# Sums on VectorE in a hybrid decoder step: the first feature pair's weight sums and the squares of x

## The chip, the cores and the metric

The kernel runs on one core of one Trainium2 chip. The metric is the device time in microseconds (us) of one execution; of several runs the median is given. In the text, PE is TensorE (PEld its weight loads), DVE is VectorE, ACT is ScalarE, POOL is GpSimd, and SP is SyncE, which here only issues DMAs.

## The reference

One layer of a conditioned decoder runs for a prompt of 1024 rows and for 8 samples of 4 rows, which the kernel joins to R = 1056 columns of a transposed x (1024 features in 8 tiles of 128 partitions). Cut to what matters here:

```python
h = rmsnorm(x, g_norm1) * (1 + scale1) + shift1
za, zq, zkv, zg, zm = jnp.split(h @ w_in, SPLIT_IDX, axis=-1)
...                                        # gMLP mixer, sparse attention, output projection
x = x + gate1 * mixed
h2 = rmsnorm(x, g_norm2) * (1 + scale2) + shift2
up = h2 @ w_up                             # 1024 -> 2 * 2816
conv = b_conv
for k in range(CONV_W):                    # causal depthwise convolution, width 3
    conv = conv + w_conv[k] * upc[:, k:k + T]
a, gv = jnp.split(conv, 2, axis=-1)
x = x + gate2 * ((jax.nn.gelu(a) * gv) @ w_down)
```

All inputs and outputs are float32. Before these lines a conditioning vector gives shift, scale and gate, and after them a last RMSNorm follows.

## The kernel before

**Precision and weights.** A float32 product is made from parts: `split` copies a tile into a rounded high part (ACT) and subtracts it for the low part (DVE), and each product of two tiles is three matmuls (high by high, high by low, low by high). A product with float32 operands, such as the row sums, leaves two records for each matmul in the trace. Weight tiles come through three rings of 128x512 buffers: `raw` (6 buffers, filled by `raw_load` on SP's queue), `hi` and `lo` (4 each). `weights(src, 8)` takes two raw buffers and two of each other ring.

**Order.** Except for PE in one part in the middle, a scheduler puts the instructions of each engine in order at build time: it runs a timeline of its own simulation (`schedule_with_timeline_sim=True`) and prefers what stands earlier in the program. Each engine then works its list off in that order, and waits on semaphores for data and for buffers.

**Statistics of x.** x is cut into three chunks of columns, CH = 0:384, 384:768, 768:1056. `x_stats(c)` squares the eight tiles of a chunk (ACT, L328), adds the squares over the features and turns the sums into factors: `row_sums` multiplies 128-column pieces of each tile handed to it with a column of ones (PE, one column of output), `rstd_rows` makes 1/sqrt by a few small DVE steps (L286 to L305), spreads them by transposes on PE (L294), and ACT copies them to RB (L333). Before `row_sums`, chunk 0's squares are added up by DVE and chunk 2's by POOL (L330) into the first tile, so that one tile is handed on; chunk 1's eight tiles are handed on as they are. `x_mult(c)` multiplies x by RB (L338; POOL for two tiles in eight, DVE for the rest), `h_tile` scales, shifts and splits the tiles (L390 to L398), and `rows(2, ...)` multiplies them with the first weights. The loop runs over the chunks: `h_tile` of chunk c, then `x_stats` and `x_mult` of chunk c + 1, then `rows` of chunk c.

**Up projection.** The 22 feature pairs (one tile of a, one of gv) are computed by a scheme of seven block products on halves of rows (HR = 528 columns), features and outputs, as in Winograd's form of fast matrix multiplication. The activations need the combined operands T1 to T4, B22 and the plain ones in BS, made once (`sums_of`, `turned`: ACT casts L1625, DVE subtracts L1626, DVE sums L1634, L1635, L1653, L1656). The weights of a pair need the sums s1 to s4 of its four raw 128x512 blocks a11, a12, a21, a22: `pair_weights(j)` loads these and `add_up` forms the sums (L1546 to L1549), on POOL for all pairs. For pair 0 the sums live in two `acc` tiles and `add_up` is called apart from the load.

Before pair 0 stands a preparation: `first_products(j)` makes two of the block products of pairs 0 to 3 ahead, with weights loaded by `weights` into `early[0]` to `early[3]`, and ACT copies them out of PSUM (L1533). Between them `sums_of` is called four times. Then `pair(j)` runs for all pairs: products with s2, s3, a22, s1 and s4 (and two more from pair 4 on), DVE adds of the banks into the tiles ua and ug (L1569, L1583, L1595 to L1598), the convolution (L1521 to L1523), gelu (L1607), a product on POOL (L1608) and the store.

Of the kernel before, what the change touches and what calls it, by code (L numbers as in the profile page):

```python
# [11 lines left out]
OP = mybir.AluOpType  # L12
# [38 lines left out]
def step_kernel(tc, A):  # L51
    nc = tc.nc
    sync, act, dve, pool, pe = nc.sync, nc.scalar, nc.vector, nc.gpsimd, nc.tensor
# [211 lines left out]
    def row_sums(pv, ts):  # L265

        w = ts[0].shape[1]
        for i in range(-(-w // 128)):
            n = min(128, w - 128 * i)
            for k, t in enumerate(ts):  # L270
                m = mm(pv[0:n, i:i + 1], t[:, 128 * i:128 * i + n], ones, k == 0, k == len(ts) - 1)
        return m
# [51 lines left out]
    def x_stats(c):  # L324
        a, b = CH[c]
        sq = [R0([128, 384], F32, "sq", 8)[:, 0:b - a] for k in range(8)]
        for k in range(8):
            act.activation(sq[k], xs[k][:, a:b], AF.Square)  # L328
            if c != 1 and k:
                (pool if c else dve).tensor_tensor(sq[0], sq[0], sq[k], op=OP.add)  # L330
        pv = pT()
        row_sums(pv, sq if c == 1 else sq[0:1])
        act.copy(RB[:, a:b], rstd_rows(None, a, b, pv)[0])  # L333

    def x_mult(c):
# [1043 lines left out]
    def parts(x):  # L1379
        n = x.shape[1]  # L1380
        hi, lo = (W([128, 512], F32R, tag, 4)[:, 0:n] for tag in ("hi", "lo"))
        split(x, hi, lo)
        return [[t[:, c:c + 128] for c in range(0, n, 128)] for t in (hi, lo)]
# [88 lines left out]
    T2, T3, T1 = ([R5([128, R], F32R) for _ in range(4)] for _ in range(3))  # L1472
# [53 lines left out]
    def first_products(j, behind=()):  # L1526

        t = slot()
        for i, bank in enumerate((pA, pU)):
            X = [bank(), bank()]  # L1530
            half_products([w[4 * i:4 * i + 4] for w in early[j]], BS[4 * i:4 * i + 4], X, behind[i:i + 1] if i == 0 else behind[1:])
            for c in range(2):
                act.copy(t[:, HR * i + HB * c:HR * i + HB * c + HB], X[c][:, 0:HB])  # L1533
        return t

    def pair_weights(j):

        a11, a12, a21, a22 = (raw_load(A["w_up"][n][:, c:c + 512]) for n in (j, 22 + j) for c in (0, 512))
        cst = R5B([128, 2, 16], F32, "cst", 2)
        for i in range(2):  # L1540
            sync.dma_start(cst[:, i], A["st_cv"][:, 22 * i + j].rearrange("p b t -> p (b t)"))
        t0, t1 = (R5B([128, RU], F32, "acc", 2) if j == 0 else slot() for _ in range(2))
        s1, s2, s3, s4 = t0[:, 0:512], t0[:, 512:1024], t1[:, 0:512], t1[:, 512:1024]

        def add_up():
            pool.tensor_tensor(s1, a21, a22, op=OP.add)  # L1546
            pool.tensor_tensor(s2, s1, a11, op=OP.subtract)
            pool.tensor_tensor(s3, a11, a21, op=OP.subtract)
            pool.tensor_tensor(s4, a12, s2, op=OP.subtract)  # L1549

        if j:
            add_up()
        return cst, (a11, a12, a22), (s1, s2, s3, s4), add_up

    def pair(j, cst, raws, sums, add_up, begun=None):

        (a11, a12, a22), (s1, s2, s3, s4) = raws, sums
        ua = up_tile()
        if begun is None:
            w11 = parts(a11)  # L1560
            X = [pA(), pA()]
            half_products(w11, BS[0:4], X)
            p1 = ua[:, 2:2 + HR]
            for o, c, c0, n in pieces(ua, 0):
                act.copy(o, X[c][:, c0:c0 + n])
        else:
            p1 = begun
            for o, c, c0, n in pieces(ua, 0):
                dve.tensor_tensor(o, p1[:, HB * c:HB * c + n], p1[:, HR + HB * c:HR + HB * c + n], op=OP.add)  # L1569
        ug = up_tile()  # L1570
        for i, u in enumerate((ua, ug)):
            pool.tensor_copy(u[:, 1026:RU].rearrange("p (b t) -> p b t", t=6)[:, :, 0:2],
                             cst[:, i].rearrange("p (b t) -> p b t", t=2))

        def product(w, x, bank):
            X = [bank(), bank()]
            half_products(w, x, X)
            return X

        def add(up, half, banks, other=None):  # L1580

            for o, c, c0, n in pieces(up, half):
                dve.tensor_tensor(o, by4(banks[c][:, c0:c0 + n], n), other(c, c0, n) if other else o, op=OP.add)  # L1583

        def of_p1(c, c0, n):
            return by4(p1[:, HB * c + c0:HB * c + c0 + n], n)

        def of_ua(c, c0, n):
            return sample_of(ua) if n == 32 else ua[:, 2 + HR + HB * c + c0:2 + HR + HB * c + c0 + n]

        w2 = parts(s2)
        add(ua, 1, product(w2, T2, pT), of_p1)
        add(ug, 1, product(parts(s3), T3, pU), of_ua)
        Y = product(parts(a22), T4, pA)
        dve.tensor_tensor(ug[:, 2:2 + HB], Y[0][:, 0:HB], ug[:, 2 + HR:2 + HR + HB], op=OP.add)  # L1595
        e = NP - HR - HB
        dve.tensor_tensor(ug[:, 2 + HB:2 + HB + e], Y[1][:, 0:e], ug[:, 2 + HR + HB:2 + NP], op=OP.add)
        dve.tensor_tensor(by4(ug[:, 2 + HB + e:2 + HR], 32), by4(Y[1][:, e:HB], 32), sample_of(ug), op=OP.add)  # L1598
        Y = product(parts(s1), T1, pT)
        add(ug, 1, Y)  # L1600
        add(ua, 1, Y)
        add(ua, 1, product(parts(s4), B22, pU))
        if begun is None:
            add(ua, 0, product(parts(a12), BS[4:8], pA))
        g = conv(22 + j, ug)
        a = conv(j, ua)
        act.activation(a[:, 0:RU - 2], a[:, 0:RU - 2], AF.Gelu_apprx_tanh)  # L1607
        pool.tensor_tensor(a[:, 0:NP], a[:, 0:NP], g[:, 0:NP], op=OP.mult)  # L1608
        sa, sg = (t[:, 1026:1026 + 48].rearrange("p (b t) -> p b t", t=6)[:, :, 0:4] for t in (a, g))
        pool.tensor_tensor(a[:, NP:R].rearrange("p (b t) -> p b t", t=4), sa, sg, op=OP.mult)  # L1610
        pool.dma_start(ff_d[j], a[:, 0:R])
        return w2[1][3]
# [16 lines left out]
    def sums_of(k):  # L1629
        h2_tile(k, *done)  # L1630
        h2_tile(4 + k, *done)
        f = slot()
        F.append((f[:, 0:HR], f[:, HR:R]))
        dve.tensor_tensor(F[k][0], b2(4 + k), b2(k), op=OP.subtract)  # L1634
        dve.tensor_tensor(F[k][1], F[k][0], b1(k), op=OP.add)  # L1635
        turned(F[k][1], T2[k])

    begun = [first_products(0, [(1, m1), (0, m1), (1, m2)])]
    sums_of(0)
    begun.append(first_products(1, [(0, m2), (0, m2), (0, m2)]))  # L1640
    sums_of(1)
    early.append(weights(A["w_up"][2], 8))
# [1 line left out]
    begun.append(first_products(2))  # L1644
    early.append(weights(A["w_up"][3], 8))
    sums_of(3)
    loaded = [pair_weights(0)]
    begun.append(first_products(3))
    loaded[0][3]()
    for k in range(4):  # L1650
        turned(F[k][0], T3[k])
    for k in range(4):
# [210 lines left out]
```

## Time and profile before

| what | value |
|---|---|
| median of 3 runs | 1980.49 us (1976.86 to 1985.71) |
| profiled execution, its own time | 1976.38 us |
| span of its trace, first to last instruction | 1974.7 us |
| PE, DVE, ACT, POOL busy | 94%, 60%, 40%, 24% of the span |
| granted TensorE clock, mean | 0.976 |
| DMA | 346.14 MB, 175 GB/s on average |

A line of a timeline gives the start in us from the span's start, the duration, engine, line of the kernel, operation, tiles out<-in (all tiles are called t), shape and count, and in brackets the idle time of that engine before it and what ended it. Consecutive instructions of a kind are merged into one line with their count. A line "A <- B: total, times, longest" says how long A's engine waited for B. L56 is the line of all matmuls but the transposes.

### The profile page before, as it was taken

The numbers are of one execution on the slowest core, as the hardware profiler recorded it, in microseconds if no ns is written. First come the engines' busy times: TensorE is split into PE (matmuls) and PEld (weight loads), VectorE is DVE, ScalarE is ACT, GpSimd is POOL, SyncE is SP. The second block draws the span as 40 slices with busy tenths as digits, with TensorE's granted clock in tenths as the row PEclk, the third lists the DMA queues.
The fourth block names the chain that finished last, engine by engine and source line by source line (L and its number), as shares of the span: only waits on it lengthen the run. The fifth ranks groups of instructions, "written<-read, shape, count | busy, mean of one in ns | idle before, by whom it ended". The sixth has DMA issues, their size and how long they took to land.

```text
span 1974.7 us, 43773 instructions
## 1 busy us (share of the span) xinstructions
PE 1853.6 (94%) x16073; PEld 1746.1 (88%) x16073; DVE 1181.3 (60%) x2536; ACT 786.8 (40%) x1602; POOL 483.7 (24%) x624
## 2 busy tenths in 40 slices
PE   6799999999998998989889999799999999999996
PEld 4799999999997776767679999789999999999996
DVE  6613421112115676676665768899999999756464
ACT  4313111112114554656551357334444444545342
POOL 3410110100000000000001411766777765201010
PEclk9799999999998999999999999899999999999998
DMA  8364656766658577677773444233322223856462
GB/s 327 97 207 129 195 184 211 243 220 201 211 171 273 178 245 234 223 230 231 232 259 136 150 164 143 76 104 105 103 98 71 73 88 95 291 188 209 137 190 89
DMA packets 253894, 346.14 MB, mean 175 GB/s; under 512 B 35280, under 2 KB 189296, under 8 KB 251504
## 3 DMA queue, kind: packets, MB, share of 16 engines
q1 hardware_dynamic: 205696, 262.91, 41.3%
q10 hardware_dynamic: 36896, 41.22, 6.5%
q0 software_dynamic: 11088, 39.21, 5.6%
q8 instruction: 127, 2.08, 0.4%
q14 instruction: 87, 0.71, 0.1%
HBM read 305.96 MB, written 41.43 MB: 176 GB/s over the span
## 4 chain that ended last, share of the span: by engine, by line
PE 76%; DVE 7%; SPq 4%; issue 4%; DMA 4%; ACT 3%; POOL 1%; DVEq 0%; ACTq 0%; POOLq 0%
PE t L56 73%; SPq L522 3%; PE t L1161 2%; DMA t<-w_ada 2%; DVE t L320 1%; DMA t<-t 1%; DVE t L1583 1%; ACT t L319 1%; POOL t L1546 1%; DVE t L1523 1%; SPq L512 1%; DVE t L1522 1%; ACT t L1165 1%; PE t L991 0%; DMA t<-psel 0%
## 5 line engine op out<-in xcount | busy, mean ns | idle before, releaser
L56 PE MATMUL t<-t,t 128*128 128x264 f32 (+12 forms) x15298 | 1777.6, 306 | 91.7 <-DVE t L173 14.8
L56 PEld LDWEIGHTS t<-t,t 128*128 128x128 f32 (+3 forms) x15138 | 1663.5, 170 | 144.3 <-issue 61.3
L320 DVE TENSOR_TENSOR t<-t,t 128x512 fp32r<-128x512 f32 (+2 forms) x478 | 386.5, 817 | 324.5 <-ACT t L319 319.5
L319 ACT CAST t<-t 128x512 fp32r<-128x512 f32 (+5 forms) x544 | 311.1, 589 | 437.5 <-PE t L56 332.3
L1583 DVE TENSOR_TENSOR t<-t,t 128x264 f32<-128x264 f32 (+2 forms) x366 | 107.3, 340 | 11.8 <-PE t L56 11.7
L1192 POOL COPY t<-t 128x256 f32<-128x256 f32 x32 | 13.1, 411 | 297.1 <-DVE t L1190 185.9
L1161 PEld LDWEIGHTS t<-t,t 128*128 128x128 f32 x528 | 58.4, 144 | 30.4 <-ACT t L1010 9.2
L1521 ACT ACTIVATE t<-t,t 128x1072 f32<-128x1072 f32 x44 | 56.6, 1286 | 60.3 <-DVE t L1583 41.7
L1165 ACT COPY t<-t 128x512 f32<-128x512 f32 (+1 forms) x112 | 58.8, 568 | 46.5 <-PE t L1161 46.3
L683 ACT ACTIVATE t<-t 128x384 f32<-128x384 f32 (+1 forms) x48 | 22.2, 465 | 136.6 <-PE t L56 115.0
L1522 DVE SCALAR_TENSOR_TENSOR t<-t,t,t 128x1072 f32<-128x1072 f32 x44 | 73.2, 1663 | 5.4 <-ACT t L1521 4.6
L1161 PE MATMUL t<-t,t 128*128 128x128 f32 x528 | 74.9, 281 | 0.7 <-DVE t L1213 0.3
L1136 ACT ACTIVATE t<-t,t 128x640 f32<-128x640 f32 (+3 forms) x64 | 56.2, 878 | 37.8 <-DVE t L1135 32.4
L1706 POOL TENSOR_TENSOR t<-t,t 128x384 f32<-128x384 f32 (+1 forms) x12 | 14.9, 1274 | 228.9 <-ACT t L1764 228.9
L1523 DVE SCALAR_TENSOR_TENSOR t<-t,t,t 128x1072 f32<-128x1072 f32 x44 | 69.7, 1584 | 0.0
L1135 DVE TENSOR_REDUCE t<-t 128x1 f32<-128x640 f32 (+3 forms) x64 | 58.9, 921 | 17.9 <-PE t L56 16.1
L1546 POOL TENSOR_TENSOR t<-t,t 128x512 f32<-128x512 f32 x22 | 47.1, 2140 | 87.6 <-DMA t<-w_up 77.0
L685 POOL DMA_DIRECT2D t<-t x16 | 8.5, 532 | 220.0 <-DVE t L684 163.9
L1608 POOL TENSOR_TENSOR t<-t,t 128x1024 f32<-128x1024 f32 x22 | 54.0, 2453 | 17.3 <-ACT t L1607 17.3
L981 DVE TENSOR_TENSOR t<-t,t 128x512 f32<-128x512 f32 x32 | 22.1, 690 | 42.7 <-PE t L56 42.6
L1402 POOL TENSOR_TENSOR t<-t,t 128x384 f32<-128x384 f32 (+1 forms) x24 | 27.9, 1165 | 71.9 <-DVE t L1401 68.7
L320 DVE TENSOR_TENSOR t<-t 128x384 fp32r<-128x384 f32 (+1 forms) x66 | 36.9, 585 | 11.7 <-ACT t L319 11.5
(282 smaller groups left out, 1275.6 us busy)
## 6 DMA issues: line engine op xcount, KB each, us to landing
t<-psel SPq DMA_DIRECT2D x512, 128.0 KB
t<-pcmp SPq DMA_DIRECT2D x332, 128.0 KB
t<-w_down SPq DMA_DIRECT2D x120, 256.0 KB
t<-t POOLq DMA_DIRECT2D x50, 528.0 KB, 4.3
t<-w_up SPq DMA_DIRECT2D x96, 256.0 KB
t<-pcmp ACTq DMA_DIRECT2D x180, 128.0 KB
t<-w_ada SPq DMA_DIRECT2D x16, 1024.0 KB
t<-w_t ACTq DMA_DIRECT2D x52, 256.0 KB
```

Source lines behind the costliest of these rows:

```text
L56: return pe.matmul(out, lhsT, rhs, start=start, stop=stop)
L319: act.copy(hi, t)
L320: dve.tensor_tensor(lo, t, hi.bitcast(F32), op=OP.subtract)
L522: d = queue.dma_start(dst, src[bass.ds(r, 1)].rearrange("g p c -> p (g c)"))
L1135: dve.tensor_reduce(m4[:, branch, h:h + 1], ps[:, :, 0:w], axis=AX.XY, op=OP.max, negate=True)
L1161: pe.transpose(pt[:, c:c + 128], probs[branch, h][:, 128 * b:128 * b + 128], ident)
L1165: (act.copy if w > 2 else dve.tensor_copy)(probs[branch, h][:, 128 * k:128 * (k + w)], pt[:, c:c + 128 * w])
L1521: act.activation(acc[:, 0:w], up[:, 0:w], AF.Identity, scale=cw[:, n, 0:1], bias=cw[:, n, 3:4])
L1522: dve.scalar_tensor_tensor(acc[:, 0:w], up[:, 1:1 + w], cw[:, n, 1:2], acc[:, 0:w], op0=OP.mult, op1=OP.add)
L1523: dve.scalar_tensor_tensor(acc[:, 0:w], up[:, 2:2 + w], cw[:, n, 2:3], acc[:, 0:w], op0=OP.mult, op1=OP.add)
L1546: pool.tensor_tensor(s1, a21, a22, op=OP.add)
L1583: dve.tensor_tensor(o, by4(banks[c][:, c0:c0 + n], n), other(c, c0, n) if other else o, op=OP.add)
```

## The change

Two places change. In `x_stats`, DVE adds up the squares of every chunk, so chunks 1 and 2 hand one tile to `row_sums` as chunk 0 does. In the feature pairs, `pair_weights(0)` (its raw loads and two small ones of convolution state) stands ahead of `early[2]` and `early[3]` in the program instead of behind them; `add_up` of pair 0 runs on DVE and is called after the first `sums_of`; and in `pair(0)` the product with s1 comes ahead of that with a22, while its addition into ug stays behind.

```diff
@@ x_stats
             act.activation(sq[k], xs[k][:, a:b], AF.Square)
-            if c != 1 and k:
-                (pool if c else dve).tensor_tensor(sq[0], sq[0], sq[k], op=OP.add)
+            if k:
+                dve.tensor_tensor(sq[0], sq[0], sq[k], op=OP.add)
         pv = pT()
-        row_sums(pv, sq if c == 1 else sq[0:1])
+        row_sums(pv, sq[0:1])
@@ pair_weights
         def add_up():
-            pool.tensor_tensor(s1, a21, a22, op=OP.add)
-            pool.tensor_tensor(s2, s1, a11, op=OP.subtract)
-            pool.tensor_tensor(s3, a11, a21, op=OP.subtract)
-            pool.tensor_tensor(s4, a12, s2, op=OP.subtract)
+            eng = pool if j else dve
+            eng.tensor_tensor(s1, a21, a22, op=OP.add)
+            eng.tensor_tensor(s2, s1, a11, op=OP.subtract)
+            eng.tensor_tensor(s3, a11, a21, op=OP.subtract)
+            eng.tensor_tensor(s4, a12, s2, op=OP.subtract)
@@ pair
         add(ug, 1, product(parts(s3), T3, pU), of_ua)
+        if j == 0:
+            Y5 = product(parts(s1), T1, pT)
+            add(ua, 1, Y5)
         Y = product(parts(a22), T4, pA)
 ...
-        Y = product(parts(s1), T1, pT)
-        add(ug, 1, Y)
-        add(ua, 1, Y)
+        if j:
+            Y = product(parts(s1), T1, pT)
+            add(ug, 1, Y)
+            add(ua, 1, Y)
+        else:
+            add(ug, 1, Y5)
         add(ua, 1, product(parts(s4), B22, pU))
@@ preparation
+    loaded = [pair_weights(0)]
     begun = [first_products(0, [(1, m1), (0, m1), (1, m2)])]
     sums_of(0)
+    loaded[0][3]()
     begun.append(first_products(1, [(0, m2), (0, m2), (0, m2)]))
     sums_of(1)
     early.append(weights(A["w_up"][2], 8))
 ...
     sums_of(3)
-    loaded = [pair_weights(0)]
     begun.append(first_products(3))
-    loaded[0][3]()
```

## The prediction

> **What bounds the kernel now.** I read the page first, then the waits of TensorE (PE), then the two stages that the diff touches: first by stretches of 4 us, then as timelines.
>
> ```profile
> span 1974.7 us, 43773 instructions
> PE 1853.6 (94%) x16073; PEld 1746.1 (88%) x16073; DVE 1181.3 (60%) x2536; ACT 786.8 (40%) x1602; POOL 483.7 (24%) x624
> PE 76%; DVE 7%; SPq 4%; issue 4%; DMA 4%; ACT 3%; POOL 1%; DVEq 0%; ACTq 0%; POOLq 0%
> PE t L56 <- ACT t L319: 12.3, 3, 10.2
> PE t L56 <- ACT t L397: 10.0, 3, 6.9
> 82.42 187.66 PE t L56 x1874
> 293.81 190.02 PE t L56 x1705
> ```
>
> PE is busy 94% of the span and carries 76% of the chain that ended last, so time is won where PE idles or does work that can go. Its two longest waits after the start-up are one of 10.2 us for a cast of L319 and one of 6.9 us for a cast of L397. The first lies in the preparation of the feature pairs, the second between the first and the second chunk of x; the diff touches just these two places. The last two lines are from the chain in order of time: from 82.42 to 484 us it is PE's own work but for 24 us, so what is won before 82 us should travel on.
>
> Stage one, the statistics of x. Columns: length, busy time (count) of PE, PEld, DVE, ACT, POOL, then granted clock, DMA share, GB/s.
>
> ```profile
> 36.00:40.00 4.00, 3.31 (x26) 2.98 (x25) 3.36 (x8) 4.00 (x10) 2.23 (x1) 1.00 1.08 362
> 40.00:44.00 4.00, 4.00 (x36) 4.00 (x34) 1.92 (x3) 3.02 (x8) 1.00 (x1) 0.91 1.04 403
> 44.00:48.00 4.00, 4.00 (x20) 4.00 (x21) 0.15 (x1) 2.94 (x7) 1.87 (x3) 0.50 0.39 155
> 48.00:52.00 4.00, 4.00 (x19) 4.00 (x20) 2.58 (x10) 0.98 (x4) 2.39 (x4) 0.50 0.01 4
> 56.00:60.00 4.00, 0.00 (x0) 0.00 (x0) 4.00 (x5) 1.93 (x3) 3.38 (x3) 1.00 0.00 1
> 68.00:72.00 4.00, 4.00 (x24) 3.79 (x23) 0.84 (x6) 0.15 (x1) 0.00 (x0) 0.68 0.00 2
> 88.00:92.00 4.00, 4.00 (x35) 4.00 (x34) 0.73 (x2) 0.63 (x1) 0.00 (x0) 1.00 0.81 252
> ```
>
> DVE is nearly idle from 44 to 48 us and from 68 to 72 us: there it waits for row sums on PE. Two rows by shape (36 to 56 us) say what PE does meanwhile, and the timeline gives the chain.
>
> ```profile
> L56 PE MATMUL t<-t,t 128*128 128x1 f32 x48 | 7.6, 292 | 0.0
> 14.82 1.41 PE L56 MATMUL t<-t,t 128*128 128x1 f32 x6 [14.82 <-DVE t L173]
> 39.62 1.75 ACT L328 ACTIVATE t<-t 128x384 f32<-128x384 f32 x4
> 48.01 0.16 DVE L286 TENSOR_SCALAR t<-t 128x3 f32<-128x3 f32 x1 [3.87 <-PE t L56]
> 50.33 0.16 DVE L305 TENSOR_TENSOR t<-t,t 128x4 f32<-128x4 f32 x1
> 54.09 0.49 PE L294 MATMUL t<-t,t 128*128 128x128 f32 x3
> 54.62 0.48 ACT L333 COPY t<-t 128x384 f32<-128x384 f32 x1 [0.59 <-PE t L294]
> 62.20 2.52 PE L56 MATMUL t<-t,t 128*128 128x262 f32 x12 [6.88 <-ACT t L397]
> 72.04 0.40 ACT L333 COPY t<-t 128x288 f32<-128x288 f32 x1 [3.89 <-PE t L294]
> 72.47 2.80 DVE L338 TENSOR_TENSOR t<-t,t 128x288 f32<-128x288 f32 x4 [3.31 <-ACT t L333]
> 79.45 1.00 PE L56 MATMUL t<-t,t 128*128 128x262 f32 x6 [2.70 <-ACT t L397]
> 82.42 27.77 PE L56 MATMUL t<-t,t 128*128 128x262 f32 x206 [1.97 <-DVE t L398]
> ```
>
> The last square of the second part is done at 41.37 (39.62 + 1.75), but its 48 row-sum records keep PE until 48 us. Then come the small DVE steps (48.01 to 50.49), and the transposes stand behind the remaining products until 54.09. PE then waits 6.88 us for the second chunk. The third part repeats the pattern: DVE waits 3.31 us for its copy at 72.04.
>
> Stage two, the first feature pair.
>
> ```profile
> 1230.84 12.97 POOL L1546 TENSOR_TENSOR t<-t,t 128x512 f32<-128x512 f32 x1 [11.29 <-DMA t<-w_up]
> 1243.78 1.25 POOL L1548 TENSOR_TENSOR t<-t,t 128x512 f32<-128x512 f32 x1
> 1246.28 1.14 ACT L319 CAST t<-t 128x512 fp32r<-128x512 f32 x2 [12.05 <-POOL t L1547]
> 1218.66 18.07 PE L56 MATMUL t<-t,t 128*128 128x264 f32 x146
> 1246.95 1.25 PE L56 MATMUL t<-t,t 128*128 128x264 f32 x4 [10.22 <-ACT t L319]
> 1289.27 20.96 PE L56 MATMUL t<-t,t 128*128 128x264 f32 x155 [4.45 <-DVE t L1583]
> 1219.40:1242.70 23.30, 17.33 (x143) 17.12 (x141) 23.30 (x57) 14.35 (x33) 12.01 (x2) 0.97 0.10 35
> 1242.70:1264.00 21.30, 15.39 (x104) 14.63 (x105) 13.20 (x19) 10.58 (x21) 11.09 (x8) 0.79 0.27 86
> 1268.00:1290.00 22.00, 16.90 (x135) 16.51 (x134) 22.00 (x35) 8.01 (x10) 20.22 (x20) 0.98 0.26 85
> ```
>
> POOL's first sum starts when its operand lands and takes 12.97 us, where the next takes 1.25. It ends 1.1 us after DVE's uninterrupted run (23.30 busy of 23.30). ACT, which works in order, has the split of s2 at the head of its queue and waits 12.05 us; behind it stand a weight cast and copies that empty PSUM, and PE stops for 10.22 us.
>
> **The change part by part.**
>
> Row sums of the second part. 48 records (7.6 us of PE) become 6, which took 1.41 us for the first part. Added are seven dependent DVE adds:
>
> ```profile
> L330 DVE TENSOR_TENSOR t<-t,t x7: 540/549/559, 8.6 to 14.1; 128x384 f32<-128x384 f32 x7
> L330 POOL TENSOR_TENSOR t<-t,t x7: 791/799/1100, 46.0 to 58.3; 128x288 f32<-128x288 f32 x7
> ```
>
> 7 x 0.549 = 3.84 us. From 36 to 44 us DVE has 8 - 3.36 - 1.92 = 2.7 us free, so the last add ends near 44.5. Row sums add 1.4 (45.9), the small steps 50.49 - 48.01 = 2.5 (48.4), the transposes 0.5; with some tenths for PE's order the copy at 54.62 comes at 49.5, 5.1 us earlier. Bounds: 6.6 if PE takes each step when it is ready (48.0), 1.3 if the row sums stand behind the rest of the first chunk's products (then only part of the 6.2 us of PE work is won); nothing below that, since PE's work only shrinks. I take 5.1, nearest to the sum of rows.
>
> The granted clock is 0.50 from 44 to 52 us, though PE is busy throughout: it falls while the one-column products run. The products after them run 19 in 4.00 us (48 to 52), where 35 run in 4.00 at clock 1.00 (88 to 92): at that pace the 19 take 2.2, 1.8 us less. This is not added; it makes 49.5 reachable. The Trainium skill, "TensorE: Matmul & The Clock Gate", Part 1, says the gate halves the clock after an idle window of some 3.4 us and that activity releases it; a PE without idle time should by that stay fast, and dropping the row sums would leave the clock alone. The trace differs (0.50 at 4.00 of 4.00 busy); by the rule alone the 1.8 us would not be won, and the copy would come near 51 (a sum of 12.2 instead of 13.7, below).
>
> Row sums of the third part. Seven POOL adds (0.80 each) become DVE adds, 0.549 x 288/384 = 0.41 each, 2.9 us, bounded by 0.41 and 0.549. They fit DVE's idle stretch of 44 to 48 us, since squares that now wait for PE to release the second part's tiles get them from the DVE adds. The factors are then ready before DVE has finished the second chunk, and the 3.31 us of waiting at 72.47 goes. Late next is DVE itself, full in 56 to 60 us. Gain 3.3, bounds 0 (the adds push the second chunk's products) and 4.7 (both PE waits before 82.42, 2.70 + 1.97, gone). POOL's own copies come earlier; nobody on PE waits for them.
>
> Sums of pair 0 by DVE. Removed: POOL's 12.97 and three of about 1.25. Added: four DVE adds, by
>
> ```profile
> 1218.80 0.69 DVE L320 TENSOR_TENSOR t<-t,t 128x512 fp32r<-128x512 f32 x1 [0.72 <-ACT t L319]
> 1228.11 0.33 SPq L1368 DMA_DIRECT2D t<-w_up  x1
> ```
>
> 0.69 each, 2.8 us, in a DVE that is full. The 10.22 us of PE and 12.05 of ACT go. But all the turned operands come from DVE, which is full in 1268 to 1290 too (22.00 of 22.00), where PE waits 4.45 us for its adds, so what counts is DVE's idle time: 21.30 - 13.20 = 8.1 us, less 2.8, is 5.3. Bounds: 10.2 (PE's wait alone) and, below nothing, the fourth rival. I take 5.3, since the stage ends on DVE.
>
> Loads of pair 0 ahead of two weight tiles. On SP's queue four loads of 256 KB and two small ones pass four others; their number is unchanged and POOL's queue gets none. Today's last of the twelve is issued at 1228.11 and lands by 1230.84; that place falls to the fourth tile's second half, whose cast and subtraction (1.14/2 + 0.69) end near 1232.1, before PE wants it at 1236.73. Cost 0; bounds 0 and 3 if its buffer is freed only by the sums. DVE's sums would wait in order for the raw loads, but these now take places five to eight of the twelve.
>
> Product with s1 ahead of a22, its second add later. Same matmuls; two PSUM banks are held over three short adds (under 1 us), while PE has 48 products for other banks. Cost 0.
>
> Sum: 5.1 + 3.3 + 5.3 = 13.7. The profiled execution took 1976.38 us for a span of 1974.7; less 13.7 it would be 1962.7. The median shown is 1980.49, 4.1 above, so the forecast for a median is 1966.8, rounded to 1967.
>
> **The rivals.**
>
> First, the stall only moves: the gain of stage one comes, that of stage two does not, because another in-order wait takes over (the fourth weight tile, ACT behind POOL for pair 1). For it: POOL is busy 20.22 of 22.00 us in 1268 to 1290. Against: its sums are short there (median 1.63 us, in the fourth rival's row). 1980.5 - 8.4 = 1972.
>
> Second, stage one's part is hidden: DVE's extra adds (3.84 + 2.9 us) set the pace and the second chunk comes no sooner. For it: DVE is full in 56 to 60 us. Against: it idles 3.85 of 4.00 at 44 to 48. 1980.5 - 5.3 = 1975.
>
> Third, neither arrives: 1980, should the scheduler (which orders by a simulated timeline) give back elsewhere what is won here.
>
> Fourth, slower. The change closes DVE's gaps, and POOL's sums for pair 1 need such gaps:
>
> ```profile
> L1546 POOL TENSOR_TENSOR t<-t,t x22: 1278/1626/12974, 1230.8 to 1646.5; 128x512 f32<-128x512 f32 x22
> ```
>
> Each sum that meets a run like that of 1230 us costs 12.97 - 1.25 = 11.7 us, with ACT's queue behind it. One costs most of the 13.7; past 13.7 us, that is a second one, the kernel is slower: two give 1980.5 - 13.7 + 23.4 = 1990; three 2002. For it: that row's maximum. Against: the median of 22 such sums is 1.63 us. The Trainium skill, "SBUF — State Buffer", Who interferes with whom, says that a DVE instruction with two SBUF inputs and a GpSimd instruction that reads SBUF exclude one another; the trace agrees, but the wait here outlasted a whole run of DVE instructions, not one.
>
> **How the numbers follow.** Both gains 0.56; first rival 0.14; second 0.10; third 0.10; fourth 0.10. Half a percent, 9.9 us, is about what a measurement of this kernel can tell from no change (its runs span 1976.86 to 1985.71). Faster by more: nearly all of the forecast and a third of the first rival, 0.58; slower by more: the fourth and a little scatter, 0.11; the rest, 0.31. Range: the low end from the upper bounds, 6.6 + 4.7 + 10.2 = 21.5, and 2 us of scatter, 1957; the high end takes in rivals one to three, 1981. The forecast's own range is 1958 to 1971.
>
> **What would show it.** Six one-column records instead of 48 near 40 us, a clock of 1.00 there, the copies of L333 near 49.5 and well before 72; PE's long run starting near 74 instead of 82.42. Near 1230 no POOL sum of pair 0 and no ACT wait for POOL; the wait of 10.22 us gone, smaller waits for DVE in its place; the run of 1289.27 some 14 us earlier. It is wrong if a sum of pair 1 lasts over 5 us, if PE waits over 3 us for the fourth weight tile, or if the gain of the first 82 us is given back by 600.

## The result

| | median us | runs | ratio to before (95% interval) |
|---|---|---|---|
| before | 1984.99 | 5 (1976.86 to 1986.36) | |
| after | 1966.25 | 5 (1964.85 to 1970.59) | 0.9916 [0.9897, 0.9934] |

The change makes the kernel faster: 16.6 us of 1980.49 by the ratio, 13.1 to 20.4 by its interval. The two profiled executions, 1976.38 and 1964.85 us, stand 11.5 apart. The forecast was 1967 us and a sum of 13.7. One execution of the experiment e5_second_eight, the profiled one, ran at a mean granted clock of 0.746 and took 2296.88 us; it is in no ratio, and that kernel was profiled a second time.

### The profile after

The head of the page (before: PE 1853.6 us busy, x16073, so 6.1 us and 42 records less):

```profile
span 1963.0 us, 43697 instructions
PE 1847.5 (94%) x16031; PEld 1740.0 (89%) x16031; DVE 1178.8 (60%) x2554; ACT 785.6 (40%) x1602; POOL 465.8 (24%) x613
```

Then TensorE's timeline from the first product with x to the long run, with ScalarE's copy of the third part's factors (L333). Of the edited places, L1546 to L1549 are L1547 to L1550 in the new file, L1583 is L1584, and L1608, L1626 and L1634 are L1615, L1633 and L1641.

```profile
34.85 6.09 PE L56 MATMUL t<-t,t 128*128 128x262 f32 x36 [0.41 <-ACT t L397]
42.18 1.00 PE L56 MATMUL t<-t,t 128*128 128x262 f32 x6 [1.24 <-ACT t L397]
44.05 8.30 PE L56 MATMUL t<-t,t 128*128 128x262 f32 x42 [0.87 <-DVE t L398]
52.28 0.54 PE L294 MATMUL t<-t,t 128*128 128x128 f32 x3
61.38 4.23 PE L56 MATMUL t<-t,t 128*128 128x262 f32 x18 [8.56 <-ACT t L397]
65.44 0.55 PE L294 MATMUL t<-t,t 128*128 128x128 f32 x3
65.92 6.87 PE L56 MATMUL t<-t,t 128*128 128x262 f32 x54
66.03 0.40 ACT L333 COPY t<-t 128x288 f32<-128x288 f32 x1 [0.59 <-PE t L294]
73.48 0.51 PE L56 MATMUL t<-t,t 128*128 128x262 f32 x2 [0.69 <-ACT t L397]
74.24 16.02 PE L56 MATMUL t<-t,t 128*128 128x262 f32 x129 [0.25 <-DVE t L398]
```

The long run begins at 74.24 instead of 82.42, 8.2 us earlier. The way there is another than forecast. TensorE resumes after the first chunk only 0.8 us earlier (61.38, was 62.20), and its wait there has grown from 6.88 to 8.56 us. The other 7.4 us come after that: from resuming to the long run 20.22 us have become 12.86. Two things are seen in it. The transposes of the third part stand behind 18 products instead of 35 (and the part's six row-sum records), so that its factors are copied at 66.03 instead of 72.04, and the waits of 0.91, 2.70 and 1.97 us have become 0.69 and 0.25.

The stretch as a whole says more plainly what was won. From the first product to the long run TensorE was busy 34.67 us before and is busy 27.78 now; its idle time has changed little, 13.15 against 11.61. Its one-column records took 8.8 us there and take 1.9. So most of the gain is work that TensorE no longer does, not waiting that has gone.

Why the second part's factors are no earlier than 52.85 is on VectorE, in TensorE's order and in the clock:

```profile
49.62 0.15 DVE L303 TENSOR_TENSOR t<-t,t 128x4 f32<-128x4 f32 x1
51.45 0.17 DVE L465 COPY t<-t 128x6 f32<-128x6 f32 x1 [1.68 <-PE t L56]
51.97 0.15 DVE L305 TENSOR_TENSOR t<-t,t 128x4 f32<-128x4 f32 x1
52.85 0.48 ACT L333 COPY t<-t 128x384 f32<-128x384 f32 x1 [0.28 <-PE t L294]
53.47 1.56 DVE L485 COPY t<-t 64x128 f32<-64x128 f32 x4
55.06 4.71 DVE L338 TENSOR_TENSOR t<-t,t 128x384 f32<-128x384 f32 x6
```

The granted clock at that time (last column but two; a full clock is 1.00):

```profile
46.00:48.00 2.00, 2.00 (x11) 2.00 (x11) 1.76 (x6) 1.03 (x4) 0.00 (x0) 0.50 0.05 18
48.00:50.00 2.00, 2.00 (x11) 2.00 (x11) 1.77 (x7) 0.00 (x0) 0.00 (x0) 0.50 0.00 0
```

Between two of the small steps (L303 and L304) the scheduler has put a copy that needs TensorE's first row tile; it costs 1.68 us of waiting, and the transposes stand behind those same products. These run at a granted clock of 0.50 with TensorE busy 2.00 of 2.00 us, although 42 of the 48 one-column records are gone. Between the factors (52.85) and the first multiplication with them (55.06), VectorE makes six copies (L485).

The second stage, TensorE and then the first and last sum on VectorE:

```profile
1209.83 4.14 PE L56 MATMUL t<-t,t 128*128 128x1 f32 x18 [3.10 <-DVE t L1430]
1248.55 22.21 PE L56 MATMUL t<-t,t 128*128 128x264 f32 x168 [2.06 <-DVE t L1584]
1273.60 6.19 PE L56 MATMUL t<-t,t 128*128 128x264 f32 x36 [2.84 <-DVE t L1584]
1206.75 0.69 DVE L1547 TENSOR_TENSOR t<-t,t 128x512 f32<-128x512 f32 x1 [0.87 <-DMA t<-w_up]
1209.69 0.69 DVE L1550 TENSOR_TENSOR t<-t,t 128x512 f32<-128x512 f32 x1
```

GpSimd's sums of L1547 for the later pairs, shortest, median and longest in ns, and TensorE's group from 1195 to 1340 us:

```profile
L1547 POOL TENSOR_TENSOR t<-t,t x21: 1274/1677/2918, 1246.4 to 1633.4; 128x512 f32<-128x512 f32 x21
```

```profile
L56 PE MATMUL t<-t,t 128*128 128x264 f32 (+1 forms) x1008 | 132.8, 294 | 12.3 <-DVE t L1584 5.5 <-DVE t L1430 3.1 <-DVE t L320 2.7
```

The stall of 10.22 us is gone. TensorE waits 12.3 us in that stretch, most of it for VectorE. The same row of the kernel before:

```profile
L56 PE MATMUL t<-t,t 128*128 128x264 f32 (+2 forms) x972 | 126.2, 291 | 18.9 <-ACT t L319 10.5 <-DVE t L1583 5.8 <-ACT t L1533 1.0
```

New is the wait of 3.10 us at 1209.83: the four sums stand on VectorE, with the wait for their weights, among the last steps of the x1 normalization. The 18 row-sum records after it take 4.14 us.

What is won early is not given back. A run of 121 products that both profiles have stands at 657.10 us before and at 646.18 after, 10.9 us earlier; in the last stage a run of 448 products is 11.9 us earlier (1896.03 and 1884.14).

### The profile page after: what moved, and what is told of

Its sections match the earlier page's. It is cut to its first block, busy times and chain, and to the rows that moved or that the text cites. A ratio compares the mean times of both kernels' runs of the same rounds, so it can differ in the third digit from the quotient of the medians.

```text
span 1963.0 us, 43697 instructions
## 1 busy us (share of the span) xinstructions
PE 1847.5 (94%) x16031; PEld 1740.0 (89%) x16031; DVE 1178.8 (60%) x2554; ACT 785.6 (40%) x1602; POOL 465.8 (24%) x613
## 4 chain that ended last, share of the span: by engine, by line
PE 77%; DVE 6%; SPq 5%; DMA 5%; issue 3%; ACT 2%; DVEq 0%; ACTq 0%
PE t L56 75%; SPq L522 4%; DMA t<-w_ada 2%; PE t L1161 2%; DVE t L320 1%; DMA t<-t 1%; SPq L512 1%; ACT t L319 1%; DVE t L1135 1%; DMA t<-psel 1%; ACT t L1136 1%; ACT t L1165 1%; DMA t<-pcmp 0%; DVE t L338 0%; DMA t<-w_rows 0%
## 5 line engine op out<-in xcount | busy, mean ns | idle before, releaser
L56 PE MATMUL t<-t,t 128*128 128x264 f32 (+11 forms) x15256 | 1772.7, 305 | 84.7 <-DVE t L173 14.8
L56 PEld LDWEIGHTS t<-t,t 128*128 128x128 f32 (+2 forms) x15096 | 1658.6, 170 | 137.8 <-issue 61.6
L320 DVE TENSOR_TENSOR t<-t,t 128x512 fp32r<-128x512 f32 (+2 forms) x478 | 390.7, 825 | 317.7 <-ACT t L319 295.7
L1584 DVE TENSOR_TENSOR t<-t,t 128x264 f32<-128x264 f32 (+2 forms) x366 | 107.4, 339 | 12.8 <-PE t L56 12.8
L1522 DVE SCALAR_TENSOR_TENSOR t<-t,t,t 128x1072 f32<-128x1072 f32 x44 | 71.6, 1627 | 10.7 <-ACT t L1521 10.1
L1523 DVE SCALAR_TENSOR_TENSOR t<-t,t,t 128x1072 f32<-128x1072 f32 x44 | 63.2, 1435 | 0.0
L1547 POOL TENSOR_TENSOR t<-t,t 128x512 f32<-128x512 f32 x21 | 35.4, 1687 | 105.0 <-DMA t<-w_up 67.3
L1615 POOL TENSOR_TENSOR t<-t,t 128x1024 f32<-128x1024 f32 x22 | 54.3, 2469 | 17.1 <-ACT t L1614 17.1
```

The costliest lines, as they stand in the source:

```text
L56: return pe.matmul(out, lhsT, rhs, start=start, stop=stop)
L320: dve.tensor_tensor(lo, t, hi.bitcast(F32), op=OP.subtract)
L1522: dve.scalar_tensor_tensor(acc[:, 0:w], up[:, 1:1 + w], cw[:, n, 1:2], acc[:, 0:w], op0=OP.mult, op1=OP.add)
L1523: dve.scalar_tensor_tensor(acc[:, 0:w], up[:, 2:2 + w], cw[:, n, 2:3], acc[:, 0:w], op0=OP.mult, op1=OP.add)
```

## The experiments

All ratios are to the kernel before on the same chip. The last three columns are lengths in us on TensorE in the profiled execution: from the first product with x (34.60 before, 34.85 after) until it resumes with the second chunk, from there to the long run, and from the first product to the run of 121 products near 650 us. By the trace the long run begins after 146 of the 262-column products in the changed kernel, 151 before and 155 in e4 and e14, so the second length compares only to a us or so. The third ends at the same work in all; kernels whose first stage is the same differ in it by up to 1.8 us.

| kernel | median us | ratio | to resuming | to the long run | to the 121 products |
|---|---|---|---|---|---|
| before | | | 27.60 | 20.22 | 622.50 |
| after | 1966.25 | 0.9916 [0.9897, 0.9934] | 26.53 | 12.86 | 611.33 |
| e1_stats_only | 1973.59 | 0.9956 [0.9939, 0.9972] | 25.99 | 12.84 | 611.52 |
| e2_pair_only | 1977.35 | 0.9972 [0.9957, 0.9987] | 26.32 | 19.97 | 620.73 |
| e3_sums_behind | 1967.47 | 0.9920 [0.9898, 0.9942] | 26.97 | 12.83 | 612.80 |
| e4_third_pool | 1970.25 | 0.9935 [0.9914, 0.9956] | 25.56 | 15.95 | 613.29 |
| e5_second_eight | 1977.82 | 0.9981 [0.9967, 0.9996] | 28.35 | 18.53 | 622.08 |
| e6_sums_pool | 1962.91 | 0.9907 [0.9889, 0.9924] | 26.43 | 12.86 | 611.58 |
| e7_late_load | 1971.01 | 0.9935 [0.9921, 0.9948] | 26.83 | 12.83 | 612.41 |
| e10_copies_behind | 1968.86 | 0.9936 [0.9918, 0.9955] | 24.71 | 17.05 | 615.32 |
| e11_filler | 1966.48 | 0.9919 [0.9900, 0.9938] | 24.87 | 12.86 | 611.26 |
| e13_own_tiles | 1977.08 | 0.9963 [0.9950, 0.9977] | 26.47 | 18.93 | 619.22 |
| e14_best_own | 1964.98 | 0.9899 [0.9883, 0.9914] | 30.55 | 14.51 | 616.45 |

The lengths in the row of e5_second_eight are from a second run of the same kernel, e5_again (a single execution, 1979.61 us).

### Each half alone

e1 takes the kernel before and changes `x_stats` only; e2 takes the changed kernel and puts `x_stats` back:

```diff
-            if c != 1 and k:
-                (pool if c else dve).tensor_tensor(sq[0], sq[0], sq[k], op=OP.add)
+            if k:
+                dve.tensor_tensor(sq[0], sq[0], sq[k], op=OP.add)
...
-        row_sums(pv, sq if c == 1 else sq[0:1])
+        row_sums(pv, sq[0:1])
```

> Only the statistics of x are changed; the feature pairs stay as before. Theory (two independent gains, some 8 us in the first 82 us and some 4 us net in the feature pairs): about 8 us less than before, a ratio of 0.996; PE's long run starts near 74 us instead of 82.42, and the wait of 10.2 us at the first pair is still there. Rival (one of the two parts brings all of it): a ratio of 0.992 here and 1.000 with the pairs alone, or the other way round.

> Only the feature pairs are changed; the statistics of x stay as before. Theory: PE's wait of 10.2 us goes, some 4 us are lost just ahead of it (the four DVE sums stand before the last residual tile), and about 4 us remain: a ratio of 0.998. Rival (one part brings all): 0.992 or 1.000.

e1's first rows, then e2's:

```profile
74.33 15.89 PE L56 MATMUL t<-t,t 128*128 128x262 f32 x128 [0.25 <-DVE t L398]
1208.79 2.41 PE L56 MATMUL t<-t,t 128*128 128x1 f32 x18 [0.96 <-DVE t L1430]
1239.93 1.25 PE L56 MATMUL t<-t,t 128*128 128x264 f32 x4 [10.20 <-ACT t L319]
```

```profile
82.61 7.56 PE L56 MATMUL t<-t,t 128*128 128x262 f32 x42 [1.96 <-DVE t L398]
1221.11 4.14 PE L56 MATMUL t<-t,t 128*128 128x1 f32 x18 [3.06 <-DVE t L1430]
```

Each half has its own gain and its own place: e1 has the early long run and keeps the stall, e2 the reverse. By the ratios e1 saves 8.7 us (5.5 to 12.1), e2 5.5 (2.6 to 8.5) of 1980.49. Their product, 0.9928, lies in the interval of both together, so the gains add up as far as these intervals tell; the one-part rivals fall. The wait of 3.1 us comes with the second half.

### Stage one: which part's adds

e4 gives the third part's adds back to GpSimd, e5 gives the second part's eight tiles back to TensorE, each with all else of the change:

```diff
 e4
-                dve.tensor_tensor(sq[0], sq[0], sq[k], op=OP.add)
+                (pool if c == 2 else dve).tensor_tensor(sq[0], sq[0], sq[k], op=OP.add)
 e5
-            if k:
+            if c != 1 and k:
...
-        row_sums(pv, sq[0:1])
+        row_sums(pv, sq if c == 1 else sq[0:1])
```

> The changed kernel, with the third part's squares added up by POOL as before; only the second part's stay on DVE. Theory A (the third part's adds on DVE sit between the small steps of the second part's chain, which took 6.0 us instead of 2.5): the copy of L333 comes near 49.6 instead of 52.85, and PE's long run starts 1 to 3 us earlier than 74.24. Theory B (the third part's factors are what the adds on DVE win): the second copy of L333 comes near 70 instead of 66.03, and PE's long run starts 2 to 4 us later, at 76 to 78.

> As the changed kernel, but the second part of x keeps its eight squares unadded, so TensorE again makes three runs of eight one-column products for it; only the third part's squares are added up by VectorE. Theory (the third part's adds on VectorE are worth nearly all of the 8.2 us of stage one; the second part's adds bring at most 1.8 us, since their small steps only spread out among the third part's adds): 1966 to 1969 us, the long run of products begins between 74.2 and 76.5 us. Rival, the split of the prediction (5.1 us from the second part): about 1971 to 1972 us, the long run at 79 to 80 us.

> The kernel with the second part's eight squares unadded and the third part's added up by VectorE once more, for a profile at the clock of the others. Theory: the third part's squares begin only when TensorE has read the second part's eight tiles, near 45 to 46 us (45.02 in the kernel before, behind a wait of 2.0 us for TensorE; 43.8 in the changed kernel, behind no wait for it); VectorE's adds for it begin after 45.5 and end after 50 us; the third part's factors are copied out near 72 us, as in the kernel before, and the long run begins at 81 to 84 us. Rival (the third part's adds on VectorE bring 3 us by themselves, as the prediction's terms have it): the copy near 69 and the long run at 79.

With e2 the four cases are complete: neither part's adds 0.9972, the third's alone (e5) 0.9981, the second's alone (e4) 0.9935, both 0.9916. The second's alone bring 0.0037, 7.3 us; the third's alone bring nothing (-0.0009, -1.8 us, within the intervals); on top of the second's they bring 0.0019, 3.8 us, with intervals that overlap. The last column of the table agrees: 7.4 us for the second's alone (620.73 to 613.29), nothing for the third's alone (622.08), and 2.0 on top of the second's (611.33), which is little more than the scatter. The expectation for e5, read from the places of L333 in one pair of timelines, had the two parts the wrong way round; the split of the prediction (5.1 and 3.3) was nearer, but for the condition.

In e4 both theories missed. The factors' copy is not early: 54.68, 17.9 us after the first product, as after the change (18.0), though the small steps now take only 3.5 us (49.02 to 52.48); the transposes follow at 53.72, behind the first chunk's products. And the third part's copy is only 0.4 us later (68.40, 31.6 us after the first product against 31.2), where 4 were expected. Before the change it came at 37.4, and in e5_again at 37.8: it is the second part's adds that bring the third part's factors forward.

```profile
54.68 0.51 ACT L333 COPY t<-t 128x384 f32<-128x384 f32 x1
```

e5_again shows what holds the third part there, ScalarE, then VectorE and TensorE:

```profile
46.30 3.40 ACT L328 ACTIVATE t<-t 128x288 f32<-128x288 f32 x8 [2.67 <-PE t L56]
68.94 0.16 DVE L305 TENSOR_TENSOR t<-t,t 128x4 f32<-128x4 f32 x1
67.54 4.66 PE L56 MATMUL t<-t,t 128*128 128x262 f32 x25 [2.63 <-DVE t L398]
72.04 0.55 PE L294 MATMUL t<-t,t 128*128 128x128 f32 x3
```

The third part's squares wait 2.67 us for TensorE, which must first read the second part's eight tiles, since both parts share eight buffers. The factors are done at 69.10, yet the transposes follow at 72.04, behind 31 products (6 and 25).

e13 takes the shared buffers out of it: e5 with other tiles for the third part's squares.

```diff
-        sq = [R0([128, 384], F32, "sq", 8)[:, 0:b - a] for k in range(8)]
+        if c == 2:
+            sq = [(KC if k < 3 else VC)[:, 288 * (k % 3):288 * (k % 3) + 288] for k in range(6)]
+            sq += [R0([128, 288], F32, "sq2", 2) for k in range(2)]
+        else:
+            sq = [R0([128, 384], F32, "sq", 8)[:, 0:b - a] for k in range(8)]
```

> The second part's eight squares unadded, the third part's added up by VectorE, and the third part's squares now in tiles of their own, so that they need not wait until TensorE has read the second part's. Theory (the wait for the tiles is why the third part's adds bring nothing without the second's): the squares begin at 42 to 43.5 us with no wait for TensorE, the third part's copy comes near 68 to 69 instead of 72 us, 1972 to 1975 us. Rival (what holds the third part is the place of its row sums and transposes in TensorE's order, and VectorE's small steps among the second part's work, which the second part's 24 one-column products delay): 1976 to 1979 us, as without the tiles.

ScalarE, VectorE and TensorE, then the clock:

```profile
42.72 0.77 ACT L332 ACTIVATE t<-t 128x288 f32<-128x288 f32 x2
44.21 2.10 ACT L332 ACTIVATE t<-t 128x288 f32<-128x288 f32 x6
66.67 0.16 DVE L305 TENSOR_TENSOR t<-t,t 128x4 f32<-128x4 f32 x1
65.28 5.13 PE L56 MATMUL t<-t,t 128*128 128x262 f32 x25 [2.53 <-DVE t L402]
70.25 0.55 PE L294 MATMUL t<-t,t 128*128 128x128 f32 x3
```

```profile
48.00:50.00 2.00, 2.00 (x11) 2.00 (x11) 1.31 (x9) 0.37 (x1) 0.00 (x0) 0.50 0.04 8
```

The squares no longer wait for TensorE (42.72 and 44.21 instead of 46.30), and the runs do not decide between theory and rival. The median, 1977.08, is in the rival's range; by the ratio the tiles save 0.0018 against e5, with intervals that overlap, and to the 121 products they save 2.9 us (619.22 against 622.08). That leaves the third part's adds 1.5 us ahead of e2, about what they bring on top of the second's, and all of this is near the scatter. What still separates e13 from the changed kernel, 7.9 us, is mainly the second part's row sums: up to the long run TensorE is busy 33.26 us here, 34.62 in e5_again, 29.03 in e4 and 27.78 in the changed kernel, and idle about 12 in each (12.14, 12.26, 12.48, 11.61). Here too the transposes stand behind 31 products and wait 3.4 us for them; in the kernels with the second part's adds they stand behind 18 (24 in e10). What that order costs was not tried by itself; no run moved these transposes alone.

### Stage one: the clock and the copies

e11 puts 17 idle products, whose result nobody reads, into TensorE's two waits at 41 to 44 us of the changed kernel (ten and seven; shown is the first place):

```diff
+                    spare = pA()[:, 0:262]
+                    for _ in range(10):
+                        with behind(held):
+                            held = [mm(spare, hh[0][:, 0:128], hi[0], True, True)]
```

> As the changed kernel, with 17 idle products (128x262, written to a spare bank that nobody reads) put into TensorE's two waits at 41 to 44 us, ten and seven, so that it doesn't stand still there. Theory (the granted clock of 0.50 at 44 to 52 us follows from the stretch of little work at 40 to 44 us): the clock is 0.9 or more at 44 to 52 us, the 42 products that took 8.30 us take 5 to 6 us, the row factors of the second part are copied 2 to 3 us earlier (50 to 51 instead of 52.85 us), TensorE resumes 2 us earlier, the time is 1 to 2.5 us under the changed kernel. Rival (the low clock has another cause, as the amount of work since the start): the clock stays at 0.50 to 0.6 at 44 to 52 us with TensorE busy all along, and the time is that of the changed kernel or up to 1 us longer.

The clock in this kernel, and the copy of the second part's factors:

```profile
46.00:48.00 2.00, 2.00 (x15) 1.72 (x14) 1.65 (x6) 1.44 (x4) 0.00 (x0) 1.00 0.10 41
48.00:50.00 2.00, 1.15 (x9) 1.04 (x9) 2.00 (x7) 0.02 (x1) 0.00 (x0) 1.00 0.00 0
```

```profile
51.70 0.48 ACT L333 COPY t<-t 128x384 f32<-128x384 f32 x1
```

The clock is 1.00 where it was 0.50, so the low clock after 44 us does follow from the waits before it; in every other run with the second part's adds, which all keep such waits, it falls to 0.55 or less there. TensorE now waits for operands instead of being late (1.15 of 2.00 us busy), and the factors come 1.8 us earlier, counted from the first product. The time is that of the changed kernel, 0.9919: a gain of 1 to 2 us is below what this comparison can tell, and in the profile nothing of it is left at the 121 products (611.26 against 611.33).

e10 queues the copies of the first two row-tile groups (L465, L485) behind the next multiplications:

```diff
-            dve.tensor_copy(G[0:n, tt, 6 * ch:6 * ch + 6], ps[:, 256:262])
+            with behind([mult[dve]] if ch == 2 and tt < 6 else []):
+                dve.tensor_copy(G[0:n, tt, 6 * ch:6 * ch + 6], ps[:, 256:262])
```

(and the same for the L485 copies)

> As the changed kernel, but the copies that move the first and second row tiles' results out (the 6-column copies and the 64x128 copies of the third projection) are queued behind the next part's multiplications by the row factor. Theory (after the second copy-out of the row factors, VectorE spends 2.2 us on six such copies before the multiplications that TensorE waits for, and 1.7 us before it waiting for TensorE's first tiles): the multiplications begin within 0.3 us of the row factors instead of 2.2 us, TensorE resumes at 58.5 to 59.5 instead of 61.4 us, the time is 1.5 to 2.5 us under the changed kernel. Rival (what TensorE then waits for is ScalarE's copies and the subtractions, or the moved copies only stand in the way later): the long run begins at 74 us as before, 1966 to 1967 us.

```profile
58.76 1.68 PE L56 MATMUL t<-t,t 128*128 128x262 f32 x6 [7.47 <-ACT t L400]
63.03 4.30 PE L56 MATMUL t<-t,t 128*128 128x262 f32 x18 [2.60 <-DVE t L401]
```

TensorE resumes 1.8 us earlier, counted from the first product, and loses it at once: after six products it waits 2.60 us for the subtractions (L401 here), among which the copies now stand, and needs 17.05 us to the long run instead of 12.86. The time, 0.9936, is on the side of the rival, and to the 121 products it takes 4.0 us more than the changed kernel: the copies only change their place.

### Stage two: the sums, their place and the load

e3 keeps VectorE's sums but orders them behind the last small step of the x1 normalization; e6 puts them on GpSimd; e7 keeps them on VectorE and loads the weights at the old place:

```diff
 e3
-    loaded[0][3]()
+    with behind(chain[-1:]):
+        loaded[0][3]()
 e6
-            eng = pool if j else dve
+            eng = pool
 e7
-    loaded = [pair_weights(0)]
     begun = [first_products(0, [(1, m1), (0, m1), (1, m2)])]
     sums_of(0)
-    loaded[0][3]()
...
     sums_of(3)
+    loaded = [pair_weights(0)]
     begun.append(first_products(3))
+    loaded[0][3]()
```

> The changed kernel, with the four DVE sums of pair 0 ordered behind the last normalization chain (its last small DVE step) instead of in front of it. Theory (the sums in front of the last residual tile cost 3.8 us: PE's idle time of 3.1 instead of 1.0 us and slow clock after it): 3 to 4 us less than the changed kernel, a ratio of 0.990 to before; PE's wait ahead of the one-column records of the third chunk under 1.5 us. Rival (DVE sets the pace from there to pair 3, so an earlier start is lost again): the same time as the changed kernel, 0.992.

> As the changed kernel, but the four sums of the first pair are made by GpSimd, which stands idle between 1204 and 1216 us; the loads stay ahead of two tiles. Theory (the early load is what ends the 10.2 us stall, and VectorE, which is the engine that pairs 0 to 3 wait for, is relieved of 2.8 us): the wait ahead of the last x1 normalization goes back from 3.1 to about 1 us, the stall stays away, and the kernel takes 1963 to 1966 us, 0 to 3 us under the changed kernel. Rival (GpSimd's sums are held back by VectorE's unbroken run, as one of pair 1 took 13 us in the kernel before and 2.9 us here): the fourth sum ends after 1240 us, TensorE waits for it in pair 0, and the time is 1970 us or more.

> As the changed kernel, but the first pair's raw weights are loaded at the old place, behind the third and fourth weight tile; their sums stay on VectorE. Theory (the earlier load is needed: with the raw weights landing at 1216 to 1231 us, VectorE's sums stand in order in the middle of its unbroken run, and the casts and products behind the second sum come late): the last x1 normalization is back to a wait of 1 us, but TensorE waits 3 us or more near 1230 to 1245, or the adds of pair 0 come later, and the time is 1967 to 1972 us. Rival (only the engine counted, GpSimd's sum of 13 us being the whole stall): the stall stays away and the 3 us ahead of the first products come back, 1962 to 1965 us.

e3, TensorE: the wait ahead of the row sums is back to 0.96 us, and a wait of 3.67 us for VectorE's adds, and smaller ones, take its place. Its time is that of the changed kernel, as the rival has it: an earlier start is lost again to VectorE.

```profile
1209.50 2.41 PE L56 MATMUL t<-t,t 128*128 128x1 f32 x18 [0.96 <-DVE t L1432]
1269.75 4.91 PE L56 MATMUL t<-t,t 128*128 128x264 f32 x28 [3.67 <-DVE t L1586]
```

e6, GpSimd, VectorE, TensorE:

```profile
1210.85 1.29 POOL L1548 TENSOR_TENSOR t<-t,t 128x512 f32<-128x512 f32 x1
1210.75 1.42 DVE L302 TENSOR_TENSOR t<-t 128x4 f32<-128x4 f32 x1
1212.21 1.56 DVE L303 TENSOR_TENSOR t<-t,t 128x4 f32<-128x4 f32 x1
1214.23 0.93 PE L294 MATMUL t<-t,t 128*128 128x128 f32 x3 [2.23 <-DVE t L305]
```

With the early load GpSimd's sums take 1.25 to 1.48 us each and none meets a long run of VectorE; the last ends at 1213.74, so the rival falls. What they cost shows on two small steps that take 0.16 us in the changed kernel and 1.42 and 1.56 here, beside GpSimd's sums. The Trainium skill, "SBUF — State Buffer", Who interferes with whom, lets only one of the two proceed when VectorE reads two operands from SBUF and GpSimd reads there too; by these rows the trace agrees, with VectorE the one that waits. The median, 1962.91, is the lowest of all, but the interval overlaps that of the changed kernel.

e7, VectorE, ScalarE, TensorE:

```profile
1230.37 0.67 DVE L1547 TENSOR_TENSOR t<-t,t 128x512 f32<-128x512 f32 x1
1238.09 0.67 DVE L1548 TENSOR_TENSOR t<-t,t 128x512 f32<-128x512 f32 x1
1238.79 2.18 ACT L319 CAST t<-t 128x512 fp32r<-128x512 f32 x4 [0.89 <-DVE t L1548]
1239.47 3.01 PE L56 MATMUL t<-t,t 128*128 128x264 f32 x12 [5.06 <-ACT t L319]
```

With the old load half of the stall remains (5.06 us), behind a second sum that comes 7.7 us after the first, and the time is 1971.01, in the range of its theory. So both edits count, and the load more than the engine: with the early load the stall is gone on either engine (e6 and the changed kernel), with the late one neither is free of it (10.20 us in e1, 5.06 here). The profiles say the same: from the run of 82 products just ahead of the first pair (1203.86 us before) to the last gelu it takes 503.78 us in e1, 498.70 here, 495.88 in the changed kernel and 493.49 in e6, though kernels with the changed pairs scatter from 493.72 to 498.26. All but e1 also have the product with s1 ahead of that with a22; no run tries that edit alone.

e14 adds the third part's own tiles (the diff of e13) to e6:

> All of the change, with the first pair's sums on GpSimd (1962.9 us so far), and the third part's squares in tiles of their own, so that they wait for no add of the second part. Theory (ScalarE's squares wait hardly 0.7 us for tiles here, so that little is left): 1961 to 1964 us, the long run at 73 to 74.5 us. Rival (the third part's factors are ready ahead of the second part's multiplications and TensorE gets its last chunk without the waits of 0.7 and 0.25 us): 1959 to 1961 us.

```profile
56.70 1.18 PE L56 MATMUL t<-t,t 128*128 128x1 f32 x6 [4.52 <-DVE t L334]
```

In its profile the small steps and copies come in another order, TensorE waits 4.52 us for the third part's last add, and the long run begins 45.06 us after the first product, where the changed kernel takes 39.39 and both expectations had less. Both its theories missed. To the 121 products it is 4.9 us behind e6 (616.45 against 611.58), and at the end of the profiles still 3.1 (spans of 1964.4 and 1961.3 us). The ratio, 0.9899, is nevertheless not above that of e6; the two intervals are too wide to show a loss of 3 us. No version is shown to beat the changed kernel.

## Why the prediction was right, and where not

**The forecast and its mechanism** held: 1967 against a median of 1966.25, two independent gains (8.4 and 5.3 forecast; 8.7 and 5.5 by the ratios of e1 and e2), the long run at 74.24 ("near 74"). That 1967 and 1966.25 lie within 1 us is partly luck: two more executions put the median before at 1984.99, 4.5 us above the base of the forecast, and by the ratio the gain is 16.6, not 13.7. In stage one the sum was right while the way to it was another. The first, second and third rivals need one gain or both to fail and fall with e1 and e2. The fourth needs a sum of pair 1 that takes over 5 us: the longest L1547 took 2.92.

**Second part's row sums, 5.1 us.** The size is borne out (7.3 us by e4 against e2, and 7.4 by their profiles), not the way, so that it fits is partly luck. The copy of the factors came at 52.85 instead of 49.5, 1.8 us earlier than before and not 5.1, and TensorE resumed 0.8 us earlier. The row sums were in time (forecast 45.9, the first small step came at 46.12), although by the prediction's own rows the last add ends near 45.1 and not 44.5: of 3.84 us, 2.7 fit before 44. Three steps behind them failed. The small steps were costed at 2.5 us as in the trace of before, but took from 46.12 to 52.12, since the third part's adds and copies stand between them. "Some tenths for PE's order" was too little: all 72 products of the first chunk stand ahead of the transposes and end at 52.28, so that factors ready at 48.4 would have waited there almost 4 us at this clock, and in e4, with quicker steps, the copy is no earlier. And the clock was expected at 1.00. What the runs show in place of the early copy is less work for TensorE, 34.67 to 27.78 us busy, and the third part's factors 6 us earlier, behind fewer products.

**The clock.** The prediction put the 0.50 at 44 to 52 us down to the one-column products and expected 1.00 without them. It was 0.50 again, after waits of 1.24 and 0.87 us with 1.00 us of work between them; with the waits filled (e11) it was 1.00. The Trainium skill, "TensorE: Matmul & The Clock Gate", Part 1, names beside a long idle window another way to a low clock, seen in another kernel: TensorE idling briefly but often between groups of products. The prediction used the first alone; the changed kernel agrees better with the second, since none of its waits there is longer than 1.24 us. The prediction's own reading holds beside it: e13 keeps TensorE busy without a gap from 34.60 to 53.12 us, with the 48 one-column records, and there the clock falls to 0.50 while these records run (at 45 to 46 us) and is 0.50 until 52. So both bring it about here, and a row that shows TensorE fully busy doesn't show a fast one. In e11 the full clock gains nothing that lasts to the 121 products. The sum that the prediction gives for the case that the low clock stays, 12.2, should be 11.9 (13.7 less 1.8).

**Third part's adds, 3.3 us.** In size it agrees on top of the second's (3.8 by the ratios, 2.0 by the profiles), but neither is clear of the scatter. In its condition it is right: the prediction said that these squares wait for TensorE to release the second part's tiles. It didn't draw the consequence that the gain is none without the other edit (e5), and that the third part's factors, for which VectorE waited 3.31 us at 72.47, come earlier mainly by the second part's adds (e4); a wait of 1.57 us for them is left.

**Sums of pair 0, 5.3 us.** The rule used, VectorE's idle time less 2.8, gave the right total (5.5 by e2; 4.4 by the profiles, 500.24 us before and 495.88 after from the run of 82 products to the last gelu). That is partly luck, since the rule leaves out a loss and, as e7 shows, the worth of the early load. Missed was the place: the sums run at 1206 to 1210, ahead of the first products, where they cost 2.1 us of wait (3.10 against 0.96) and 1.7 of slower row sums (4.14 against 2.41). e3 shows that moving them gains nothing.

**Loads ahead, 0 us.** No wait for the fourth weight tile is seen, as forecast. But the edit was priced as a cost only; e7 puts its worth at some 4 us (0.9935 against 0.9916, intervals that overlap). The product with s1 ahead of a22 was priced at 0 too, and no run tests that.

## To carry to other kernels

When several engines share an in-order stage, a gain forecast from one engine's idle time can be right in sum while each step is late: check what else the scheduler will put between the small steps, and which instruction of the next stage stands behind which products. Compare the engine's busy time as well as its waits: here most of the first gain was work that TensorE no longer did. Where two parts share buffers, try the four combinations before putting the gain down to either; reading one pair of timelines gave the wrong one here. An early load can be worth more than the choice of the engine that uses it.

## Of the hardware

- In the changed kernel the granted clock fell to 0.50 after two TensorE waits of 1.24 and 0.87 us and was 0.50 from 46 to 50 us with TensorE fully busy; with 17 idle products in these waits (e11) it was 1.00.
- In e13, without any wait, it fell while 48 records with one output column ran (1.00 at 42 to 44 us, 0.50 at 46 to 52).
- Two steps with two operands on 128x4 values took 1.42 and 1.56 us on VectorE beside GpSimd's sums (e6), and 0.16 without (the changed kernel).
